# Even mixer of a two-layer backbone: other rates for the work woven into five stages, two modulation pieces one stage later, and the solve's 64-product groups in two rounds

## The chip, the cores and the metric

The kernel runs on one core of one Trainium2 chip. TensorE (PE; its weight loads are PEld), VectorE (DVE), ScalarE (ACT), GpSimd (POOL) and SyncE (SP, which here only issues DMAs) each work through their own instructions in order. The metric is the device time of one execution in microseconds, lower is better. Times are medians of several executions.

## The reference, cut to what matters

The network has two layers. The first is the even layer, with the mixer that the change is in; after each mixer comes a mixture of experts. All numbers are fp32.

```python
mod = silu(c) @ ada_w[i] + ada_b[i]            # 6144 modulation columns for each layer, same for c_ctx
h = rmsnorm(x) * (1 + sc1) + sh1
p = h @ ev_w_in                                # k, v, r, low-rank decay and rate, pool input u
# for each of 8 heads, both directions, context then latent tokens:
S_t = S_{t-1} (diag(w_t) - kk_t^T (a_t kk_t)) + v_t^T k_t ;  y_t = S_t r_t
y = concat([(group_norm(yf + yb) + bonus) * g, pool_mixer(u)]) @ ev_w_out
x = x + g1 * y
```

## The kernel before, in words

The even mixer handles 512 tokens (256 context, 256 latent). The recurrence is computed in 8 chunks of 64 tokens, for two *halves* (4 heads each) and two directions d, so there are four *units* (half, d). For each unit, `ev_prep` makes decays and the products within each chunk, `ev_solve` inverts the triangular 64x64 block of every chunk, and `ev_chain` carries the state through the 8 chunks. Around them are projections of h with `ev_w_in` (`ev_k`, `ev_r`, `ev_v`, `ev_u`), pieces of the modulation (`ev_ada`: one piece is 512 of the columns of `ada_w`, 2 MB in two tiles), transposes (`ev_turn`) and the last steps (`ev_norm`, `ev_bonus`, `ev_pool`, `ev_first`, `ev_last`).

Nothing is scheduled by a compiler: each engine executes in the order in which the Python program issues. Every step is a generator, and a `yield` ends its turn. `weave` (line 109) sets the order. A *round* gives every main generator of a stage one turn, in the order in which they are listed, and then `per` turns, on average, to the *fill*, the generators of the second list, one after the other. When all main generators have ended, what is left of the fill runs alone. `STAGES` (line 356) lists eight stages; each has its main list, its fill, its `per`, and the PSUM banks for the fill and for side products. Two stages never overlap in the program's order.

One turn of `ev_k`, `ev_r`, `ev_v` or `ev_u` is two of eight products of 128x128 by 128x512 (L545). One piece of `ada` (line 261) has three turns with work on TensorE: the first tile (A, L269), the second tile and its copy to SBUF (B, L269, L275), and a small product that turns or picks the result (C, L280 or L289 and L291); what remains of a gate's piece is a DMA by POOL in its next turn. The weight tiles of all fills come in one order (`plan_even` reads the same `STAGES`) through a ring of three slots of 1 MB: when a tile is used up, SP issues the next load.

`ev_solve` goes through 15 rows, two at a time: products with a selection matrix (L802), then per row a multiply and a reduction on VectorE (L808, L809), each row waiting for the one before. Then come four groups of products through `products` (line 821): P1 and P2 with four blocks (64 products, 128 recorded matmuls and 128 weight loads, L825), P3 and P4 with two blocks (64 recorded matmuls). P2 needs a ScalarE copy of P1's result, P3 a VectorE subtraction and transpose of P2's, P4 a copy of P3's. `ev_chain` has three turns for each chunk: *a* (L871, L874, L879 and a ScalarE copy R), *b* (L883, then VU by ScalarE and VectorE, L884 and L885), *c* (L890, L903, then on VectorE the new state ZB, L897, which the next *a* needs at L874). `ev_prep` has 13 turns for each of two quarters: w, a, upto (L690, L697, L703), KB, Kh, RK (VectorE, L720 to L737), an empty one, two transposes (L743), four products (L752, L755).

Of the kernel before, what the change touches and what calls it, by code (L numbers as in the profile page):

```python
# [206 lines left out]
class Kernel:  # L207
# [96 lines left out]
    def mix_in(self, tp, pp, L, x, cols, ahead):  # L304
# [31 lines left out]
        for k in range(8):  # L336
# [11 lines left out]
            if k:  # L348
# [6 lines left out]

    STAGES = (((("kk", 0),), (("k", 0), ("r", 0)), 1.25, "fpPcC", "s"),
              ((("prep", 0, 0),), (("v", 0), ("ada", 1), ("turn", 0), ("ada", 2)), 0.8, "fcC", "s"),
              ((("prep", 0, 1), ("solve", 0, 0), ("bonus", 0)), (("ada", 6),), 1, "fc", "C"),
              ((("chain", 0, 0), ("kk", 1), ("solve", 0, 1)), (("ada", 2), ("k", 1), ("r", 1)), 1, "fp", "P"),
              ((("chain", 0, 1), ("prep", 1, 0)), (("v", 1),), 0.9, "fs", "s"),  # L360
              ((("norm", 0), ("solve", 1, 0), ("prep", 1, 1)), (("ada", 3), ("turn", 1), ("ada", 4)), 1, "fc", "C"),
              ((("solve", 1, 1), ("chain", 1, 0), ("bonus", 1), ("pool",)), (("ada", 1), ("u",), ("ada", 1)), 1, "fp", "P"),
              ((("weights",), ("end",)), (("first",), ("last",)), 0.67, "fpP", "s"))

    def plan_even(self):
# [394 lines left out]
    def ev_solve(self, half, d):  # L760

        nc, c, wp, pp = self.nc, self.c, self.wp, self.pp
        u = self.unit[half, d]
        e, l = (0, 1) if d == 0 else (1, 0)
        G = 16

        KK = u["KK"].rearrange("p (t j) g i -> p t j g i", j=2)
        side = lambda P, a, s: KK[64 * a + P.start:64 * a + P.stop, :, 1 - a, :, s]
        E, Lt = slice(32 * e, 32 * e + 32), slice(32 * l, 32 * l + 32)
        flat = lambda a: a.rearrange("p g i -> p (g i)")  # L770
        both = lambda a, P: a[P].rearrange("p (t g) i -> p t g i", t=4)
        off = lambda P, a: slice(64 * a + P.start, 64 * a + P.stop)
        AT = wp.tile([128, 512], F32, name="AT").rearrange("p (g i) -> p g i", g=G)
        for a in range(2):
            for n, P in enumerate((E, Lt)):
                (nc.scalar.copy if n else nc.vector.tensor_copy)(out=both(AT, off(P, a)), in_=side(P, a, P))
        A32 = wp.tile([128, 512], F32, name="A32").rearrange("p (g i) -> p g i", g=G)
        nc.vector.transpose(flat(A32), flat(AT))
        yield

        nc.scalar.activation(AT[:, :, 16 - 16 * d:32 - 16 * d], AT[:, :, 16 - 16 * d:32 - 16 * d], AF.Copy, scale=c["subcol"][:, d:d + 1])
        nc.gpsimd.memset(AT[:, :, 16 * d:16 * d + 16], 0.0)


        eye = c["eye16"][:, None, :].to_broadcast([128, G, 16])
        A16 = wp.tile([128, G, 16], F32, name="A16")
        nc.vector.scalar_tensor_tensor(A16, A32[:, :, 0:16], c["subcol"][:, 0:1], eye, op0=ALU.mult, op1=ALU.subtract)
        nc.vector.scalar_tensor_tensor(A16, A32[:, :, 16:32], c["subcol"][:, 1:2], A16, op0=ALU.mult, op1=ALU.add)
        X = wp.tile([128, G, 16], F32, name="X")
        nc.scalar.copy(out=X, in_=eye)  # L790
        yield
        yield
        rows = list(range(1, 16) if d == 0 else range(14, -1, -1))
        while rows:
            two, rows = rows[:2], rows[2:]
            ps = pp.tile([128, 2, G, 16], F32, name="s")
            span = lambda i: slice(0, i + 1) if d == 0 else slice(i, 16)
            for j, i in enumerate(two):
                r = span(i)
                for k in range(4):  # L800
                    Q = slice(32 * k, 32 * k + 32)
                    nc.tensor.matmul(ps[Q, j, :, 0:r.stop - r.start], c[f"sel{i}"][Q], A16[Q, :, r], start=j == 0, stop=i == two[-1],  # L802
                                     skip_group_check=True)
            for j, i in enumerate(two):
                r = span(i)
                n = r.stop - r.start
                tmp = wp.tile([128, G, 16], F32, name="tmp")
                nc.vector.tensor_tensor(tmp[:, :, 0:n], ps[:, j, :, 0:n], X[:, :, r], op=ALU.mult)  # L808
                nc.vector.tensor_reduce(X[:, :, i], tmp[:, :, 0:n], axis=AX.X, op=ALU.add)  # L809
                yield  # L810

        TT = wp.tile([128, 512], F32, name="TT").rearrange("p (g i) -> p g i", g=G)
        TN = wp.tile([128, 512], F32, name="TN").rearrange("p (g i) -> p g i", g=G)
        sub = c["sub2"].rearrange("p (s i) -> p s i", s=2)
        nc.scalar.activation(TT[:, :, 16:32], X, AF.Copy, scale=c["subcol"][:, 1:2])
        nc.vector.tensor_tensor(TT[:, :, 0:16], X, sub[:, None, 0, :].to_broadcast([128, G, 16]), op=ALU.mult)
        nc.vector.transpose(flat(TN), flat(TT))
        yield
        yield

        def products(P, L, R, blocks):
            ps = pp.tile([128, G, 32], F32, name="s")
            for g in range(G):
                for lhs, rhs, out in blocks:
                    nc.tensor.matmul(ps[out, g], L(lhs, g), R[rhs, g], start=g == 0, stop=g == G - 1, skip_group_check=True)  # L825
            return ps

        quarters = [(slice(32 * k, 32 * k + 32),) * 3 for k in range(4)]
        ps = products(None, lambda P, g: AT[P, g], TN, quarters)
        M = wp.tile([128, 512], F32, name="A32").rearrange("p (g i) -> p g i", g=G)  # L830
        nc.scalar.copy(out=M, in_=ps)
        yield
        ps = products(None, lambda P, g: M[P, g], TT, quarters)
        nc.vector.tensor_tensor(TT, TT, ps, op=ALU.subtract)
        nc.vector.transpose(flat(TN), flat(TT))
        for a in range(2):
            nc.scalar.copy(out=side(Lt, a, Lt), in_=both(TT, off(Lt, a)))
        yield
        yield

        ee, ll = ([off(P, a) for a in range(2)] for P in (E, Lt))
        ps = products(None, lambda P, g: KK[P, g // 4, 1 - P.start // 64, g % 4, Lt], TN, [(ee[a], ee[a], ll[a]) for a in range(2)])
        M = wp.tile([128, 512], F32, name="A32").rearrange("p (g i) -> p g i", g=G)
        for a in range(2):
            nc.scalar.copy(out=M[ll[a]], in_=ps[ll[a]])
        yield
        ps = products(None, lambda P, g: M[P, g], TT, [(ll[a], ll[a], ee[a]) for a in range(2)])
        for a in range(2):
            nc.scalar.copy(out=side(E, a, E), in_=both(TT, ee[a]))
            nc.vector.tensor_scalar(side(E, a, Lt), both(ps, ee[a]), -1.0, None, op0=ALU.mult)  # L850
        yield
# [1748 lines left out]
```

## Time and profile before

| | us |
|---|---|
| median of the executions shown (1870.68 to 1872.27) | 1871.91 |
| the profiled execution | 1874.16 |
| its span, first to last instruction | 1872.4 |
| of it, the five stages whose rates change (126.2 to 480.6) | 354.4 |

Stages are counted from 1, as they are listed in `STAGES`. In the trace, the third (prep 0,1; solve 0,0) lies at 126.2 to 187.1 us, the fourth (chain 0,0; solve 0,1) at 187.1 to 261.9, the fifth (chain 0,1; prep 1,0) at 261.9 to 325.4, the sixth (norm 0; solve 1,0; prep 1,1) at 325.4 to 400.9, the seventh (solve 1,1; chain 1,0; pool) at 400.9 to 480.6; each begins with the first product of its first main step. The page gives busy shares of every engine in 40 equal slices of the span (46.8 us each) and, below them, the TensorE clock that was granted. A row of the timeline has start, duration, engine, line, operation, tiles, count, and in brackets how long the engine was idle before it and what ended that; "issue" there means that the engine waited for nothing that the profile shows.

### The profile page before, as it was taken

How to read it: one execution, taken by the hardware profiler on the slowest of the kernel's cores; microseconds unless marked ns; L12 is line 12 of the kernel's file. 1: busy time of each engine (PE TensorE's matmuls, PEld its weight loads, DVE VectorE, ACT ScalarE, POOL GpSimd, SP SyncE). 2: the span in 40 equal slices, each digit the busy share in tenths (PEclk: the TensorE clock that was granted, in tenths of full speed). 3: DMA queues.
4: the chain of work that ended last, by engine and by line, in shares of the span. 5: the costliest groups of instructions: out<-in, count | busy, mean ns of one | idle time of the engine just before them, and what ended most of it. 6: DMA issues, size and time to landing. Idle time of an engine off the chain costs nothing. (4 is left out here: it accounts for less than half of the span.)

```text
span 1872.4 us, 31604 instructions
## 1 busy us (share of the span) xinstructions
PE 1637.9 (87%) x12958; PEld 933.3 (50%) x12958; DVE 817.3 (44%) x1622; ACT 447.0 (24%) x945; POOL 139.5 (7%) x170
## 2 busy tenths in 40 slices
PE   5988999989998999999999997999987787776667
PEld 2755556454776444444444433888754333332222
DVE  2564434544358245555555456665562212221113
ACT  3442222421213211111111112544421111111001
POOL 1021000103115000000000003200010000000001
PEclk8998987879898999999999997999988899898888
DMA  9275300652243879999999990622699998999996
GB/s 319 82 239 191 113 24 23 216 172 92 85 146 141 350 283 386 399 385 390 390 401 379 399 386 12 198 68 85 259 369 413 415 415 318 414 414 414 366 400 253
DMA packets 127284, 505.76 MB, mean 270 GB/s; under 512 B 11317, under 2 KB 38945, under 8 KB 85986
## 3 DMA queue, kind: packets, MB, share of 16 engines
q1 hardware_dynamic: 120946, 493.96, 68.1%
q0 software_dynamic: 3488, 8.26, 1.4%
q8 instruction: 143, 2.34, 0.5%
q10 hardware_dynamic: 2640, 0.65, 0.2%
q14 instruction: 67, 0.55, 0.1%
HBM read 501.73 MB, written 1.10 MB: 269 GB/s over the span
## 5 line engine op out<-in xcount | busy, mean ns | idle before, releaser
L1979 PE MATMUL b<-w,ht 128*64 128x512 f32 x512 | 118.8, 604 | 8.6 <-PEq L2197 8.2
L2004 DVE TENSOR_TENSOR tmp<-b,g 128x512 f32<-128x512 f32 x128 | 87.6, 686 | 70.1 <-PE b L2002 69.2
L1958 PE MATMUL b<-w,xh 128*64 128x512 f32 x512 | 116.9, 599 | 0.0
L1958 PE MATMUL b<-w,xg 128*64 128x512 f32 x512 | 116.9, 599 | 0.0
L2287 PE MATMUL b<-w,x 128*32 128x256 f32 x1024 | 77.8, 430 | 31.7 <-DMA w<-moe_w_up 14.9
L2006 DVE TENSOR_TENSOR x<-x,tmp 128x512 f32<-128x512 f32 x124 | 90.1, 726 | 4.3
L2287 PE MATMUL b<-w,xg 128*32 128x256 f32 x1024 | 74.0, 420 | 19.1 <-DMA w<-moe_w_up 14.4
L1987 DVE TENSOR_TENSOR yl<-b,yh 64x512 fp32r<-64x512 f32 x62 | 42.7, 688 | 101.4 <-ACT yh L1986 101.4
L2304 PE MATMUL b<-w,ht 128*32 128x256 f32 x1024 | 71.2, 415 | 16.6 <-ACT ht L2299 12.4
L2292 DVE SCALAR_TENSOR_TENSOR low<-b,gs,low 64x256 f32<-64x256 f32 x32 | 15.7, 490 | 157.6 <-ACT low L2291 157.6
L1979 PEld LDWEIGHTS b<-w,ht 128*64 128x64 f32 x512 | 41.6, 138 | 84.0 <-issue 72.5
L1962 ACT ACTIVATE low<-b 64x512 f32<-64x512 f32 x33 | 19.4, 588 | 253.9 <-PEq L2197 221.0
L2453 DVE COPY y<-b 32x256 f32<-32x256 f32 x62 | 25.9, 418 | 119.6 <-PE b L2304 106.3
L2287 PEld LDWEIGHTS b<-w,x 128*32 128x32 f32 x1024 | 37.1, 122 | 69.5 <-DMA w<-moe_w_up 20.6
L1986 ACT CAST yh<-b 64x512 fp32r<-64x512 f32 x62 | 36.0, 581 | 127.8 <-PE b L1979 104.6
L1963 DVE SCALAR_TENSOR_TENSOR low<-b,gs,low 64x512 f32<-64x512 f32 x32 | 36.1, 1127 | 67.2 <-ACT low L1962 67.2
L1958 PEld LDWEIGHTS b<-w,xh 128*64 128x64 f32 x512 | 33.9, 136 | 62.6 <-issue 62.0
L1958 PEld LDWEIGHTS b<-w,xg 128*64 128x64 f32 x512 | 33.9, 136 | 62.3 <-issue 61.3
L2291 ACT ACTIVATE low<-b 64x256 f32<-64x256 f32 (+1 forms) x36 | 14.4, 399 | 209.9 <-PEq L2501 130.4
L2287 PEld LDWEIGHTS b<-w,xg 128*32 128x32 f32 x1024 | 36.0, 120 | 53.3 <-DMA w<-moe_w_up 19.5
L2002 PE MATMUL b<-yh,oht 128*128 128x512 f32 (+1 forms) x128 | 58.3, 456 | 3.2 <-DVE tmp L2004 3.2
L1374 PE MATMUL b<-w,hH 128*128 128x256 f32 x320 | 59.4, 286 | 0.0
(868 smaller groups left out, 3115.5 us busy)
## 6 DMA issues: line engine op xcount, KB each, us to landing
w<-moe_w_gate SPq DMA_DIRECT2D x128, 1024.0 KB
w<-moe_w_up SPq DMA_DIRECT2D x128, 1024.0 KB
w<-moe_w_down SPq DMA_DIRECT2D x128, 1024.0 KB
w<-ada_w SPq DMA_DIRECT2D x48, 1024.0 KB
w<-od_w_in SPq DMA_DIRECT2D x12, 1024.0 KB
w<-ev_w_in SPq DMA_DIRECT2D x8, 1024.0 KB
w<-ev_w_out SPq DMA_DIRECT2D x5, 1024.0 KB
w<-od_w_out SPq DMA_DIRECT2D x4, 1024.0 KB
```

Of the source, the lines that this page charges most:

```text
L1374: nc.tensor.matmul(ps[:, t], l[:, k, T], r[:, k], start=t == 0 and k == 0 and i == 0, stop=k == 7 and i == 2, skip_group_check=True)
L1958: nc.tensor.matmul(ps[64 * j:64 * j + 64], xe(k), w[j][:, k % 4], start=k == 0, stop=k == 7)
L1963: nc.vector.scalar_tensor_tensor(hs[64:128].rearrange("s k q -> s q k"), ps[64:128].rearrange("s (q k) -> s q k", k=4), gs, sg[64:128].rea ...
L1979: nc.tensor.matmul(ps[64 * j:64 * j + 64], ht[:, k], w[:, k % 2, 512 * j:512 * j + 512], start=k == 0, stop=k == 3)
L1986: nc.scalar.copy(out=yh[:, j], in_=pj)
L1987: nc.vector.tensor_tensor(yl[:, j], pj, yh[:, j].bitcast(F32), op=ALU.subtract)
L2002: nc.tensor.matmul(ps, ohT[0:n, t], y[0:n, j], start=i == 0, stop=i == len(parts) - 1)
L2004: nc.vector.tensor_tensor(tmp, ps, g2[seg[t]][:, 512 * j:512 * j + 512], op=ALU.mult)
L2006: (nc.gpsimd if j in aside else nc.vector).tensor_tensor(xs, xs, tmp, op=ALU.add)
L2287: nc.tensor.matmul(ps[groups[j]], xe(k), w[j // 2][:, k % 4, 256 * (j % 2):256 * (j % 2) + 256], start=k == 0, stop=k == 7, skip_group_che ...
L2304: nc.tensor.matmul(ps[groups[j]], ht[:, k % 2, S * (k // 2):S * (k // 2) + S], w[:, k % 2, 256 * j:256 * j + 256], start=k == 0, stop=k == ...
L2453: (nc.scalar.copy if j % 2 else nc.vector.tensor_copy)(out=out, in_=ps[groups[j]])
```

## The change

Stages three to seven get another `per`, so that their fill lasts for more rounds. Two pieces of `ada` (layer 1, pieces 1 and 2: column pieces that no DMA writes out, first read in the odd mixer) go from the head of the fourth stage's fill to the end of the fifth's; the weight stream's order follows. And `products` becomes a generator: with more than two blocks it yields once halfway, so P1 and P2 take two rounds each; P3 and P4 stay as they are. No arithmetic and no transfer is added or removed.

```diff
-              ((("prep", 0, 1), ("solve", 0, 0), ("bonus", 0)), (("ada", 6),), 1, "fc", "C"),
-              ((("chain", 0, 0), ("kk", 1), ("solve", 0, 1)), (("ada", 2), ("k", 1), ("r", 1)), 1, "fp", "P"),
-              ((("chain", 0, 1), ("prep", 1, 0)), (("v", 1),), 0.9, "fs", "s"),
-              ((("norm", 0), ("solve", 1, 0), ("prep", 1, 1)), (("ada", 3), ("turn", 1), ("ada", 4)), 1, "fc", "C"),
-              ((("solve", 1, 1), ("chain", 1, 0), ("bonus", 1), ("pool",)), (("ada", 1), ("u",), ("ada", 1)), 1, "fp", "P"),
+              ((("prep", 0, 1), ("solve", 0, 0), ("bonus", 0)), (("ada", 6),), 0.65, "fc", "C"),
+              ((("chain", 0, 0), ("kk", 1), ("solve", 0, 1)), (("k", 1), ("r", 1)), 0.6, "fp", "P"),
+              ((("chain", 0, 1), ("prep", 1, 0)), (("v", 1), ("ada", 2)), 0.5, "fs", "s"),
+              ((("norm", 0), ("solve", 1, 0), ("prep", 1, 1)), (("ada", 3), ("turn", 1), ("ada", 4)), 0.82, "fc", "C"),
+              ((("solve", 1, 1), ("chain", 1, 0), ("bonus", 1), ("pool",)), (("ada", 1), ("u",), ("ada", 1)), 0.8, "fp", "P"),
...
             for g in range(G):
+                if g == G // 2 and len(blocks) > 2:
+                    yield
                 for lhs, rhs, out in blocks:
...
-        ps = products(None, lambda P, g: AT[P, g], TN, quarters)
+        ps = yield from products(None, lambda P, g: AT[P, g], TN, quarters)
...
-        ps = products(None, lambda P, g: M[P, g], TT, quarters)
+        ps = yield from products(None, lambda P, g: M[P, g], TT, quarters)
```

The two-block calls get the same `yield from`. Counted from the yields of the generators, with the round of the last fill turn:

| stage | rounds before | fill turns, last in round | rounds after | fill turns, last in round |
|---|---|---|---|---|
| third | 27 | 18, in 18 | 28 | 18, in 28 |
| fourth | 26 | 22, in 22 | 28 | 16, in 27 |
| fifth | 27 | 8, in 9 | 27 | 14, in 26, one behind the main steps |
| sixth | 27 | 23, in 23 | 28 | 23, in 27, one behind the main steps |
| seventh | 26 | 22, in 22 | 29 | 22, in 28 |

## Rows read from the trace of the kernel before

**Rows 1.** The page's 40 slices: TensorE's busy tenths, then its granted clock.
```profile
PE   5988999989998999999999997999987787776667
...
PEclk8998987879898999999999997999988899898888
```

**Rows 2.** Busy time of each engine in the five stages (first line names the columns).
```profile
core 0: us, PE busy (x) PEld busy (x) DVE busy (x) ACT busy (x) POOL busy (x), PEclk, DMA share, GB/s
126.20:187.10 60.90, 50.59 (x808) 30.60 (x808) 35.23 (x74) 19.59 (x37) 9.51 (x17) 0.87 0.65 221
187.10:261.90 74.80, 70.96 (x962) 39.37 (x961) 33.78 (x87) 17.47 (x38) 0.36 (x2) 0.93 0.27 86
261.90:325.40 63.50, 60.41 (x447) 40.63 (x445) 26.21 (x57) 16.73 (x35) 2.35 (x5) 0.80 0.06 18
325.40:400.90 75.50, 66.30 (x887) 38.60 (x886) 38.04 (x80) 27.29 (x48) 6.94 (x13) 0.79 0.58 196
400.90:480.60 79.70, 74.37 (x957) 39.27 (x956) 35.63 (x86) 19.57 (x43) 21.27 (x35) 0.91 0.41 132
```

**Rows 3.** The same view of the six stretches with the clock at half.
```profile
165.00:171.80 6.80, 4.07 (x97) 2.60 (x101) 5.07 (x11) 1.09 (x2) 0.00 (x0) 0.50 0.38 144
178.60:192.30 13.70, 13.70 (x185) 9.34 (x186) 7.03 (x14) 5.02 (x11) 0.36 (x2) 0.50 0.12 28
257.10:270.80 13.70, 12.39 (x146) 7.69 (x141) 2.10 (x4) 5.48 (x9) 0.00 (x0) 0.50 0.06 24
308.30:339.10 30.80, 29.94 (x145) 19.56 (x146) 11.88 (x25) 8.64 (x19) 1.21 (x3) 0.50 0.19 62
383.40:403.90 20.50, 19.13 (x305) 13.96 (x305) 7.60 (x14) 6.74 (x13) 0.67 (x2) 0.50 0.25 82
468.80:485.80 17.00, 15.78 (x217) 11.30 (x212) 3.79 (x8) 7.12 (x14) 4.46 (x7) 0.50 0.51 153
```

**Rows 4.** TensorE's waits, 126.2 to 480.6: total us, times, longest.
```profile
PE s L825 <- issue: 8.5, 3, 4.2
...
PE C L920 <- DVE sq L916: 4.3, 2, 3.7
...
PE p L752 <- issue: 1.6, 1, 1.6
```

**Rows 5.** Timeline of TensorE: P2 in the sixth, seventh and fourth stage.
```profile
384.77 1.49 PE L825 MATMUL s<-TT,A 32*32 32x32 f32 x93 [4.23 <-issue]
...
468.11 0.50 PE L825 MATMUL s<-TT,A 32*32 32x32 f32 x35 [3.24 <-issue]
...
250.17 1.29 PE L825 MATMUL s<-TT,A 32*32 32x32 f32 x128
```

**Rows 6.** DMA queues inside the stall, 380.6 to 384.7: packets, MB, share.
```profile
q1 hardware_dynamic: 651, 1.28, 93.5%
q8 instruction: 1, 0.02, 1.7%
```

**Rows 7.** The same between P1 and P2 of the fourth stage, 246.9 to 250.2.
```profile
q8 instruction: 1, 0.02, 2.3%
```

**Rows 8.** Timeline of TensorE: two hand-overs of the chain, fifth stage without fill.
```profile
305.96 0.65 PE L890 MATMUL C<-VU,tok 128*64 128x64 f32 x6 [1.09 <-ACT VU L884]
...
308.53 0.70 PE L874 MATMUL c<-ZB,RK 128*64 128x128 f32 x4 [1.18 <-DVE ZB L897]
```

**Rows 9.** Timeline of TensorE: second row pair of the solve, third and sixth stage.
```profile
136.41 0.45 PE L802 MATMUL s<-A,const_sel 32*32 32x64 f32 x16 [1.29 <-DVE tmp L808]
...
344.07 0.46 PE L802 MATMUL s<-A,const_sel 32*32 32x64 f32 x16 [1.69 <-DVE tmp L808]
```

**Rows 10.** Timeline of TensorE: one fill turn of a projection, one of `ada`.
```profile
206.42 1.98 PE L545 MATMUL f<-x,w 128*128 128x512 f32 x4
...
129.30 1.06 PE L269 MATMUL f<-w,sT 128*32 128x512 f32 x8
```

More of the change, by code (lines that the diff above doesn't have):

```diff
@@ L841, in ev_solve @@
         ee, ll = ([off(P, a) for a in range(2)] for P in (E, Lt))
-        ps = products(None, lambda P, g: KK[P, g // 4, 1 - P.start // 64, g % 4, Lt], TN, [(ee[a], ee[a], ll[a]) for a in range(2)])
+        ps = yield from products(None, lambda P, g: KK[P, g // 4, 1 - P.start // 64, g % 4, Lt], TN, [(ee[a], ee[a], ll[a]) for a in range(2)])
         M = wp.tile([128, 512], F32, name="A32").rearrange("p (g i) -> p g i", g=G)
@@ L846, in ev_solve @@
         yield
-        ps = products(None, lambda P, g: M[P, g], TT, [(ll[a], ll[a], ee[a]) for a in range(2)])
+        ps = yield from products(None, lambda P, g: M[P, g], TT, [(ll[a], ll[a], ee[a]) for a in range(2)])
         for a in range(2):
```

## Prediction

> **What bounds the kernel now.** I began with the 40 slices [rows 1]. Slices three to eleven hold the stages that change. TensorE is busy 8 to 9 tenths there, so at first sight it is full; but the clock line below it dips to 7 and 8, so part of "busy" is the same work at half speed. Next I cut the span at the stage borders [rows 2]. In 354.4 us TensorE is busy 322.6 and idle 31.8; no other engine passes six tenths of a stage (VectorE in the third: 35.2 of 60.9), and the DMA share is 0.65 at most. So TensorE's order bounds all five stages, in two ways: gaps, and the clock. For the clock I took the six stretches at 0.50 [rows 3]: TensorE is busy 95.0 us in them, of which 5.2 lie after 480.6. At full speed the 89.8 us inside would be some 45. The same work without gap and at full clock would take 322.6 - 44.9 = 277.7 us: the five stages lose 76.7 us, 31.8 to gaps and 44.9 to the clock. This is what the change can draw on. What follows (last mixer stage, experts, odd layer) depends on the end of the seventh stage, so a gain here should reach the end one to one.
>
> Then the causes. Each drop of the clock follows gaps that lie close together, at places where the fill has run out or the solve's products run: 3.7 us before L920 ahead of 165.0 [rows 4]; an "issue" wait of 1.6 us at L752, and shortly before it one of 1.0 at L825 (8.5 less the two of [rows 5]), ahead of 178.6 [rows 4]; two gaps of 1.09 and 1.18 us around 305 to 308.5 ahead of 308.3, in rounds with no fill [rows 8]; 4.23 and 3.24 us inside P2 ahead of 383.4 and 468.8 [rows 5]. Single gaps of 1.29 and 1.69 us [rows 9] were followed by no drop.
>
> **Part 1, the instruction stalls.** "Issue" waits at L825 and L752 are 8.5 + 1.6 = 10.1 us [rows 4]. In the one of 4.23 us, the instruction queue moved a single packet of 0.02 MB while the weight queue held 93.5% of the DMA engines [rows 6]; in the fourth stage the same packet went out between P1 and P2 with nothing else in flight, and P2 ran through in 1.29 us [rows 5, 7]. I read this as TensorE running out of instructions: P1 and P2 are 256 instructions each in 1.3 us, and the next block comes late behind weight loads. Halving P1 and P2 puts a round between groups of 128, some 2.3 us (60.9 us over 27 rounds in the third stage). That slows the demand to about half, but a block that takes 4 us or more to come is not covered wholly. I take 5 us of the 10.1 as gained; bounds 0 and 9.
>
> The Trainium skill, in "Runtime: NRT & Kernel Launch", section "Instruction fetch mechanics", says that instructions are fetched ahead in blocks of 16 KB and that this stays hidden, since dispatch is slower than the fetch. The trace of before does not agree: the wait of 4.23 us holds just such a packet [rows 5, 6]. By the page, nothing of this part is gained; that is the third rival.
>
> **Part 2, gaps in rounds that now get fill.** Fourth stage, rounds 23 to 26: its whole idle time, 74.8 - 71.0 = 3.8 us [rows 2], lies almost all there. Afterwards fill turns of 1.98 us [rows 10] stand in rounds 24, 26 and 27 and cover the copies between P2, P3 and P4: I leave 0.5. Fifth stage, rounds 10 to 27: idle 63.5 - 60.4 = 3.1 us [rows 2]; half the rounds get a turn: 1.5 left. Seventh: of its 5.3 us [rows 2], 3.2 are part 1, some 1.2 are P4 and the chain after round 22: 0.5 left. Sum: 5 us gained; bounds 2 and 6. The 3.7 us before L920 stay: there VectorE works without a break on prep's KB and Kh and the solve's last rows, and the round behind Kh has no fill either way.
>
> **Part 3, gaps in rounds that lose their fill.** The fill that is spread is taken from the rounds that had one each. Cover goes where nothing else stands behind a hand-over of the chain: after *b* (wait for VU, 1.09) or *c* (wait for ZB, 1.18) [rows 8]. Counting rounds, those are in the fourth stage 5, 15 and 20 in full, 3, 8 and 23 in part (some 4.7 us), in the fifth 5 (17 is in part 2), in the seventh 11: 7 us. After *a*, L879 covers the copy. In the third and sixth stage the second row pair waits for VectorE [rows 9]; VectorE's work there is unchanged, so taking one turn of 1.06 us [rows 10] away adds at most that, and where TensorE got there earlier for having less to do, less. I take 1 us for both. Sum: 8 us lost; bounds 3 and 14. The two `ada` pieces only change stage: the same TensorE work, no POOL DMA, no early reader, and in the fifth stage, whose DMA share is 0.06 [rows 2], room for their four loads. The weight loads on SP keep their order of use; those for the mixer's last stage queue behind tiles that are used later than before, but several rounds still lie between. I cost this at 0; without that cover it would be one 1 MB load, under 5 us at the 221 GB/s of the third stage [rows 2], which the range has room for. The turns left behind the main steps (fifth and sixth stage) are TensorE work at its usual price.
>
> **Part 4, the clock.** Half of the busy time in [rows 3] is lost: 2.0, 6.9, 6.2, 15.0, 9.6 and 7.9, sum 47.5 us (2.6 after 480.6). No row says which drops go, so this is bounded by counting drops. The shortest full ones lasted 13.7 us and cost up to 6.9 [rows 3]. Those at 257.1 and 308.3 follow tails without fill and should go, and the second, 30.8 us long and begun in rounds of short products alone, should at least be shorter, with turns of `ada` among them. Those at 383.4 and 468.8 go if part 1's stalls become short. The one at 165.0 stays. New ones may come where prep's VectorE work and a thinned fill meet: rounds 5 to 7 of the third, 5 to 8 of the sixth stage. I take four drops of 6.9 afterwards, the one at 165.0 among them: 27.4 in place of 47.5, so 20 us gained; bounds 0 (seven drops) and 34 (two).
>
> **Sum.** -5 - 5 + 8 - 20 = -22 us. Against the profiled execution (span 1872.4, its own time 1874.16, so 1.8 outside the span): 1852. The median of the runs shown is 2.25 below that time: 1850. With the favourable ends but few new gaps (-5, -6, +5, -34): -40, 1832.
>
> **Rivals.** First, slower: *the clock falls at every prep.* Mechanism: in rounds KB and Kh of `ev_prep`, VectorE has some 3 us and more of work for a solve or chain that TensorE waits for; until now each round had a fill turn in front of that wait. With two turns in three rounds (one in two in the fifth stage) the gaps [rows 8, 9] double up and each pair ends in a drop. For it: [rows 8], where two gaps close together did this. Against it: 1.69 alone did not [rows 9]. Price: eight drops (two each in third, fifth and sixth stage, the two P2) x 6.9 = 55 in place of 47.5, new gaps 14, gained 5 + 4: +12, about 1884. It decides from the point where more than six or seven drops remain.
>
> Second, no change: *the idle time only moves.* Gaps return one for one (part 3 at 14, parts 1 and 2 at 10), and the drops move with them, saving less than one: 1872, give or take 3.
>
> Third, *the split does nothing*: the waits come from something else, or the blocks still come too late. Then the 10.1 us stay, and so do the drops at 383.4 and 468.8. I had counted 5 us and, of those two drops, about 9: -22 + 14 = -8, 1864. For it: the weight queue fills the DMA engines for the whole stall [rows 6], and a split does not change what it loads. Against it: the quiet fourth stage, where the packet came in time [rows 5, 7]. The page of the Trainium skill named in part 1 would lead here too: fetch that is always hidden leaves the split nothing to hide.
>
> That the change doesn't do what it says is excluded by the round counts: the fill ends in the last rounds of each stage.
>
> **Chances.** Forecast case (1832 to 1862) 0.61; slower 0.17; no change 0.10; the split does nothing 0.12. A measurement of this kernel can tell about 0.2%, 4 us, from no change. Faster: 0.61 + 0.12 = 0.73; same 0.10; slower 0.17. For the range, I leave out the best end of the forecast case (0.07, below 1830) and most of the slower case (0.13, above 1874): 1830 to 1874.
>
> **What would show it.** Part 1: "issue" waits at L825 under 6 us in sum, and none above 3. Part 2: no gap over 0.7 us behind P2 in the fourth stage. Part 3: new gaps of about 1.1 us at L890 and L874 in rounds 5, 15 and 20 of the fourth stage. Part 4: half-clock time from 126 us to the end of the seventh stage of 50 to 60 us in place of 97; 257.1 and 308.3 without a counterpart. The prediction is wrong if half-clock time stays above 80 us, if VectorE's share rises above two thirds in the third or sixth stage with TensorE waiting for it, or if the experts start earlier by the gain and the end does not move.

## The result, and the profile after

| | us |
|---|---|
| before, median of 4 executions | 1871.30 |
| the changed kernel, median of 4 (1884.83 to 1889.46) | 1887.32 |
| ratio | 1.0093 [1.0068, 1.0117] |
| its profiled execution, and its span | 1884.83, 1883.0 |
| measured again beside 35 executions of before, 12 executions | 1880.27, ratio 1.0066 [1.0039, 1.0093] |

The kernel became slower by 0.7 to 0.9%, 12 to 17 us by the ratios, where 22 us of gain had been forecast. The forecast of 1850 and its range are both missed. A few executions of the experiments ran in a much slower state (two of one kernel, and one of the last, its profiled one) and are left out of every figure.

Lines from 821 on stand two lower in the code (L825 is now L827, L920 L922, L2311 L2313). First the busy time of each engine in the five stages, in the same columns as [rows 2]:

```profile
core 0: us, PE busy (x) PEld busy (x) DVE busy (x) ACT busy (x) POOL busy (x), PEclk, DMA share, GB/s
129.00:199.40 70.40, 56.55 (x808) 32.00 (x808) 36.14 (x78) 19.80 (x37) 10.42 (x17) 0.80 0.55 181
199.40:271.20 71.80, 67.37 (x904) 37.89 (x904) 31.71 (x81) 15.85 (x35) 0.35 (x2) 0.91 0.08 26
271.20:341.00 69.80, 62.41 (x502) 39.04 (x501) 27.79 (x61) 18.30 (x39) 2.35 (x5) 0.90 0.23 76
341.00:408.40 67.40, 58.97 (x887) 33.07 (x887) 38.98 (x83) 27.26 (x49) 6.37 (x12) 0.90 0.66 221
408.40:484.60 76.20, 71.72 (x950) 36.54 (x950) 32.77 (x81) 17.24 (x39) 17.53 (x29) 0.96 0.35 118
```

The third stage, with the same 808 matmuls, takes 70.4 us in place of 60.9; the sixth is 8 us shorter; the fifth holds the moved `ada` pieces (502 matmuls, 455 before). Here the borders are the first products of the main steps; by that rule the fifth stage before begins at 261.3 us and the eighth at 479.4, where [rows 2] have 261.9 and 480.6. Over all five, 355.6 us, TensorE is busy 317.0 us and idle 38.6; before, with the same borders, it is 353.2, 321.9 and 31.3. So some clock was gained, but idle time grew.

The half-clock stretches, to be held against [rows 3]:

```profile
140.90:144.30 3.40, 3.40 (x10) 0.70 (x10) 2.68 (x7) 0.00 (x0) 0.00 (x0) 0.50 0.00 0
168.20:175.10 6.90, 5.67 (x74) 2.18 (x77) 3.53 (x7) 0.64 (x2) 1.15 (x2) 0.51 0.27 73
181.90:205.80 23.90, 21.20 (x284) 13.68 (x271) 8.01 (x17) 7.04 (x14) 1.48 (x4) 0.50 0.29 93
236.50:243.30 6.80, 6.56 (x43) 3.55 (x44) 4.25 (x9) 2.48 (x4) 0.00 (x0) 0.50 0.26 99
...
sum 75.30, PE 69.95 PEld 35.05 DVE 27.68 ACT 17.31 POOL 3.78; mean PE 7.77 PEld 3.89 DVE 3.08 ACT 1.92 POOL 0.42
```

There are nine, 75.3 us in sum (97 within the five stages before). In this profile the long ones at 308 and 383 have gone, and the one at the end of the third stage has grown from 13.7 to 23.9 us.

Second, a place that the prediction did not look at: the last 35 us, far behind the change. TensorE's timeline of after, then of before:

```profile
1842.02 3.49 PE L1818 MATMUL b<-xh,const_ident 128*128 128x512 f32 x6
1851.02 0.66 PE L2313 MATMUL b<-const_ident,oh 128*128 128x128 f32 x2 [5.51 <-PEq L2503]
1852.14 0.47 PE L2300 MATMUL b<-const_ident,low 64*128 64x64 f32 x2 [0.46 <-ACT oht L2314]
1852.97 3.64 PE L2306 MATMUL b<-w,ht 128*32 128x256 f32 x32 [0.35 <-ACT ht L2301]
```

```profile
1842.48 0.41 PE L2311 MATMUL b<-const_ident,oh 128*128 128x128 f32 x2 [0.30 <-PEq L2501]
1843.41 0.30 PE L2298 MATMUL b<-const_ident,low 64*128 64x64 f32 x2 [0.52 <-ACT oht L2312]
1844.07 1.93 PE L2304 MATMUL b<-w,ht 128*32 128x256 f32 x32 [0.36 <-ACT ht L2299]
```

L2503 is the conditional around a skipped expert; "PEq" is TensorE's sequencer. The branch takes 5.51 us in place of 0.30, and the 32 matmuls behind it run at half clock (3.64 us in place of 1.93). From that product to the end of the span it takes 32.0 us (29.9 before). So 5.2 + 2.1 = 7.3 us are lost here, though nothing was changed here. Inside the gap the DMA queues moved this:

```profile
q1 hardware_dynamic: 381, 2.22, 98.4%
q8 instruction: 1, 0.02, 1.2%
```

It is the picture of [rows 6]: one instruction packet behind a full weight queue.

### The profile page after: what moved, and what is told of

Read it like the earlier page. It is cut to its first block, busy times and chain, and to the rows that moved or that the text cites. A ratio compares the mean times of both kernels' runs of the same rounds, so it can differ in the third digit from the quotient of the medians.

```text
span 1883.0 us, 31599 instructions
## 1 busy us (share of the span) xinstructions
PE 1641.9 (87%) x12958; PEld 926.2 (49%) x12958; DVE 816.2 (43%) x1622; ACT 447.1 (24%) x945; POOL 140.8 (7%) x170
## 5 line engine op out<-in xcount | busy, mean ns | idle before, releaser
L2289 PE MATMUL b<-w,xg 128*32 128x256 f32 x1024 | 75.6, 431 | 16.5 <-DMA w<-moe_w_up 13.7
L2306 PE MATMUL b<-w,ht 128*32 128x256 f32 x1024 | 75.6, 443 | 13.3 <-ACT ht L2301 12.5
```

What stands on the lines that cost most here:

```text
L2289: nc.tensor.matmul(ps[groups[j]], xe(k), w[j // 2][:, k % 4, 256 * (j % 2):256 * (j % 2) + 256], start=k == 0, stop=k == 7, skip_group_che ...
L2306: nc.tensor.matmul(ps[groups[j]], ht[:, k % 2, S * (k // 2):S * (k // 2) + S], w[:, k % 2, 256 * j:256 * j + 256], start=k == 0, stop=k == ...
```

## The experiments

Theory: the loss has two places, the branch in the tail (where the instructions lie in their blocks) and the third stage (fill taken from where it was free). Rivals: the tail waits for data; the drops of the clock merely move between stages; the split itself costs. Each kernel ran beside 31 to 35 executions of the kernel before on its own chip. Drains stand in for missing instructions: the change makes TensorE's program five instructions shorter (26,415 instructions of TensorE are recorded before, weight loads included, and 26,410 after), and they are put behind the even mixer.

| kernel | executions | median us | ratio to before |
|---|---|---|---|
| changed, five drains | 12 | 1877.57 | 1.0045 [1.0026, 1.0065] |
| before, 251 drains | 10 | 1879.30 | 1.0051 [1.0027, 1.0074] |
| split alone | 12 | 1872.11 | 1.0018 [0.9996, 1.0040] |
| all rates, no split | 12 | 1877.64 | 1.0043 [1.0023, 1.0063] |
| rates 4 to 7, no split | 12 | 1871.69 | 1.0024 [1.0001, 1.0047] |
| the same again | 10 | 1875.12 | 1.0058 [1.0031, 1.0085] |
| rates 4 to 7 and split (third put back) | 12 | 1863.44 | 0.9972 [0.9950, 0.9994] |
| changed, third at 0.8 | 12 | 1867.20 | 0.9997 [0.9974, 1.0020] |
| changed, third early | 12 | 1863.53 | 0.9973 [0.9951, 0.9995] |
| third at 0.65 alone | 11 | 1876.16 | 1.0046 [1.0020, 1.0072] |
| third at 0.65 and split | 9 | 1881.56 | 1.0070 [1.0045, 1.0096] |
| rates 6 and 7 and split | 12 | 1865.76 | 0.9987 [0.9966, 1.0007] |
| third put back, fourth 0.7 | 12 | 1863.63 | 0.9970 [0.9948, 0.9992] |
| the same, sixth and seventh 0.9 | 12 | 1863.15 | 0.9969 [0.9950, 0.9988] |
| third early, fourth 0.7, sixth 0.9 | 12 | 1860.78 | 0.9966 [0.9945, 0.9987] |

Executions of one kernel differ by 10 to 25 us here, so verdicts rest on ratios and on lengths seen in many profiles, never on the end time of one profile.

### The tail: numbers of instructions

```diff
 x = K.even(xp, seg)
 consts = ctx.enter_context(tc.tile_pool(name="consts2", bufs=1))
+for _ in range(5):
+    tc.nc.tensor.drain()
```

> The changed kernel, with five extra one-instruction drains of TensorE between the even mixer and the first experts, so that every later TensorE instruction has the same number in the program as in the kernel before. Theory 'layout': the 5.51 us gap of TensorE behind a skipped expert in the last 30 us is an instruction block that is not yet there at a branch target, and comes only from the shift by five instructions. Then the gap falls to under 1 us (before: 0.30), the half clock after it goes, and the time falls from 1887 by about 7, to 1880 (profiled against profiled: 1885 to 1878); the even mixer stays as it is. Rival 'weights': the gap has to do with data that arrive late, and comes back whatever the numbering: 1887, gap 4 to 6 us.

Measured: 1.0045, and TensorE's timeline at that place:

```profile
1853.46 0.41 PE L2313 MATMUL b<-const_ident,oh 128*128 128x128 f32 x2 [0.30 <-PEq L2503]
1854.39 0.30 PE L2300 MATMUL b<-const_ident,low 64*128 64x64 f32 x2 [0.52 <-ACT oht L2314]
1855.05 1.93 PE L2306 MATMUL b<-w,ht 128*32 128x256 f32 x32 [0.35 <-ACT ht L2301]
```

Five instructions that compute nothing remove the gap and the half clock behind it. The theory holds; "weights" falls.

The opposite, in the kernel before, at the start of the program:

```diff
+for _ in range(251):
+    tc.nc.tensor.drain()
 dp = ctx.enter_context(tc.tile_pool(name="mod", bufs=1, space=bass.MemoryType.DRAM))
```

> The kernel before with 251 one-instruction drains of TensorE at its very start, where TensorE waits until 8.96 us for its first data: every later TensorE instruction is then numbered, within blocks of 256, as behind the even mixer of the changed kernel (251 = 256 - 5). Theory 'layout': the gap behind the skipped expert (0.30 us before, 5.51 after) becomes 4 to 6 us with half clock behind it, and the time rises by about 7, plus what the drains delay the first product: 1868 to about 1876. Rival 'the even mixer's change brings the gap about': the gap stays at 0.30 us and the time at 1868 to 1870.

Measured: 1.0051, and

```profile
1838.75 0.66 PE L2311 MATMUL b<-const_ident,oh 128*128 128x128 f32 x2 [5.54 <-PEq L2501]
```

The gap appears in a kernel whose mixer was not touched. So it belongs to the position of the branch in the instruction stream: 5 fewer and 251 more do the same, as blocks of 256 instructions (or of a divisor of it) would make them. Other shifts were not tried. In all 14 profiles in which TensorE has as many recorded instructions as before, the branch takes 0.30 us. From the end of the seventh stage to the end of the span it takes 1398.4 to 1399.3 us in the three profiles with the gap and 1384.2 to 1393.0 in the others, so the loss is not given back at another branch. Such waits are no oddity of this place, though: the kernel before, too, waits 5.5 us for TensorE's sequencer at one product (L2287, 122 us before its end), and each of the 17 profiles has 7 to 12 such waits of over 1 us behind the mixer. The Trainium skill, "Runtime: NRT & Kernel Launch", section "Instruction fetch mechanics", says that a taken branch to a target outside the fetched window has to wait for a DMA fetch; the traces agree (the gap of 5.51 us holds an instruction packet, the one of 0.30 us before holds none, both beside a full weight queue), and put the price at 5.2 us here.

> The changed kernel itself, beside the same runs of the kernel before as the other three, since the difference to its copy with five drains (ratio 1.0045) is so far taken across chips. Theory 'the shifted instruction numbers cost the difference': ratio 1.008 to 1.010, gap behind the skipped expert 5 to 6 us, against 0.30 in the other three. Rival 'the first comparison overstated it': ratio 1.004 to 1.006 in spite of the gap.

The changed kernel unaltered. Measured: 1.0066, between the two theories; the gap is there (5.67 us). The interval reaches from 1.0039 to 1.0093, so by medians alone the shift costs 0.2 to 0.5%; the 7.3 us of the trace are 0.4%.

### The third stage

```diff
-(("bonus", 0)), (("ada", 6),), 0.65, "fc", "C"),
+(("bonus", 0)), (("ada", 6),), 1, "fc", "C"),
```

> The changed kernel with the third stage's rate put back to 1 (as before), the other four stages as changed; one drain keeps the instruction numbers behind the even mixer as before. Theory 'VectorE-bound rounds need their fill early': the third stage goes from 70.4 us back to about 61, its waits of 2.65 us behind the row pair and of 4.11 us at the end shrink to at most 1.5 and 3.7, and with the gap of the last 30 us gone too, the time is 1887 - 7 - 9 = 1871, a little below the kernel before if its first start is equal. Rival 'the drops only move': the third stage gains 9 and the fourth loses most of it: 1876 to 1880.

Measured: 0.9972, 5 us below the kernel before; the stage takes 59.5 us. Against the changed kernel with drains (1.0045) that is 0.73%, 13.6 us, for one number. To see why, cut the stage at its second product of `sq` (L920, L922; `sq` is made in round 18, behind Kh, and used in round 20). Before, then after:

```profile
126.20:167.70 41.50, 33.93 (x382) 16.81 (x382) 27.52 (x63) 14.22 (x28) 9.51 (x17) 0.97 0.94 323
167.70:187.10 19.40, 16.66 (x426) 13.79 (x426) 7.72 (x13) 5.37 (x9) 0.00 (x0) 0.68 0.01 3
```

```profile
129.00:169.40 40.40, 30.04 (x326) 15.12 (x326) 27.36 (x62) 12.98 (x25) 9.01 (x15) 0.94 0.67 225
169.40:199.40 30.00, 26.51 (x482) 16.87 (x482) 8.78 (x17) 6.81 (x12) 1.41 (x3) 0.61 0.39 120
```

Up to that product TensorE has 56 matmuls less to do (326 in place of 382; six fill turns: four of eight matmuls at 1.06 us [rows 10] and two short ones, some 6 us), yet gets there only 1.1 us sooner. The second part gets those 56 matmuls and is 10.6 us longer, at clock 0.61. TensorE's timeline names what held the first part:

```profile
139.30 0.45 PE L802 MATMUL s<-A,const_sel 32*32 32x64 f32 x16 [2.65 <-DVE tmp L808]
...
169.43 2.08 PE L922 MATMUL C<-sq,const_heads 128*128 128x512 f32 x2 [4.11 <-DVE sq L918]
```

The second row pair starts 10.28 us after the stage's first product (139.30 - 129.02); before, it was 136.41 - 126.17 = 10.24 [rows 9]. In 16 of the 17 profiles read it is 10.24 to 10.29 (10.56 at rate 0.8), however much fill stands ahead of it. VectorE, with ScalarE, sets that time: in after it stands still twice on the way, both times for ScalarE,

```profile
130.84 0.43 DVE L694 TENSOR_SCALAR lw<-lw 128x512 f32<-128x512 f32 x1 [1.00 <-ACT lw L693]
...
136.68 0.69 DVE L725 TENSOR_TENSOR KB<-th,kT 128x512 f32<-128x512 f32 x1 [1.07 <-ACT th L724]
```

and the wait of TensorE grew from 1.29 to 2.65. So the fill of the first 18 rounds had been nearly free, and a turn that is moved behind them has to be paid for. By the clock of the trace, the 10.6 us of the second part are 5.7 us of moved work at full clock, 4.1 us lost to the clock (20.8 us of TensorE's busy time there are at half clock, 12.6 before) and 0.8 us of idle time.

```diff
-(("bonus", 0)), (("ada", 6),), 1, "fc", "C"),
+(("bonus", 0)), (("ada", 6),), 0.65, "fc", "C"),
```

(In the kernel before; the second of the two also has the split.)

> The kernel before with the third stage's rate at 0.65 alone (no split, nothing else changed; four drains keep the later numbers). Theory 'the third stage costs by itself': it is 8 to 11 us longer (61.0 before), and the time 1.004 to 1.007 of before. Rival 'without the split it costs little': 1.000 to 1.003, the stage at 65 us or less, or given back in the fourth.

> The kernel before with the third stage's rate at 0.65 and the split, all other rates as before; four drains. Theory 'the effects add': split alone 1.0018, third stage 0.7% on top: 1.006 to 1.010. Rival 'with its fill spread over the halves the third stage is no loss': 1.000 to 1.003.

Measured: 1.0046 and 1.0070; the stage takes 71.4 and 72.6 us. Without the split, the first:

```profile
127.10:167.30 40.20, 29.83 (x326) 15.12 (x326) 27.39 (x62) 12.98 (x25) 9.04 (x15) 0.94 0.65 227
167.30:198.50 31.20, 27.04 (x482) 17.30 (x482) 8.77 (x16) 6.81 (x12) 1.41 (x3) 0.61 0.36 116
```

The same split into 40 and 31 us: the third stage costs by itself, and both theories that said so hold. Over the six profiles with 0.65 the stage takes 66.6 to 72.8 us (mean 70.7), over nine with 1 it takes 59.3 to 62.9 (mean 60.2).

```diff
-(("bonus", 0)), (("ada", 6),), 0.65, "fc", "C"),
+(("bonus", 0)), (("ada", 6),), 0.8, "fc", "C"),
```

> The changed kernel with the third stage's rate at 0.8 in place of 0.65 (1 before): its 18 fill turns end in round 23, not 28 or 18; two drains keep the later numbers. Theory 'thinned fill in front of VectorE's row pairs costs by degrees': the third stage takes about 65 us (61 at 1, 67 to 73 at 0.65) and the time lies midway, 1867 to 1873. Rival 'any thinning brings the clock down early in the stage': as at 0.65, 1875 to 1879. Rival 'only the last rounds matter': as at 1, 1861 to 1865.

Measured: 0.9997 and 64.6 us: by degrees.

```diff
+    n = 0
     while main:
         main = [g for g in main if next(g, end) is not end]
-        due += per
+        n += 1
+        due += per if per != 0.65 else 1 if n <= 6 else 0.56
```

> The changed kernel, with the third stage's fill one turn a round for the first six rounds, as before, and then thin (0.56 a round) to the last round 28; seven drains keep the later numbers. Theory 'the third stage loses at its first row pairs, where VectorE is late': the early waits (2.65, 1.15, 0.71 and 0.63 us, the drop at 137 to 144 us) shrink to those of before (1.29 and 0.55), the stage takes 61 to 63 us, and the time is near that of the third stage put back, 1862 to 1866. Rival 'it loses in its last rounds, where the clock stays down for 14 to 27 us': the early waits shrink but the stage still takes 65 us and more: 1870 to 1875.

Measured: 0.9973, with 62.5 us, cut at the same product:

```profile
130.00:170.90 40.90, 33.07 (x334) 15.90 (x334) 27.47 (x62) 13.07 (x25) 8.41 (x15) 0.85 0.69 231
170.90:192.50 21.60, 18.70 (x474) 13.22 (x474) 8.67 (x17) 6.72 (x12) 1.12 (x2) 0.82 0.58 185
```

The total came out as forecast, but not by the way that was named: the first part is as long as ever, the wait at the second row pair only went to 1.90, and only eight matmuls more were done by then. What is shorter is the second part, 21.6 us at clock 0.82: the last drop began at 188.9 us, 18.0 us behind the `sq` product (12.5 in after). One profile stands behind this; why the drop came later is open. It also bounds what the moved work explains: five of the six turns still lie behind the `sq` product here, and over twelve executions nothing is lost (0.9973, beside 0.9972 with the stage put back). So moving the turns is not enough for the loss; the time at half clock behind them belongs to it, and what sets that is not shown.

### Split and rates

```diff
-                if g == G // 2 and len(blocks) > 2:
-                    yield
```

(Taken out for "no split"; for "split alone" kept, with the rates of before.)

> The kernel before with the split of the 64-product groups alone; all rates and the two ada pieces as before. Its TensorE program is as long as that of the kernel before, so the last 30 us should show no new gap under any theory. Theory 'instruction supply': the issue waits inside P1 and P2 (8.5 us at this line before) fall under 2, the drops of the clock behind them (at 383 and 468 us) go, and the time falls by 8 to 14, to about 1860. Rival 'gaps only': the waits go, but the clock falls anyway a little later because the rounds around it are thin: 1865 to 1869. Rival 'no effect': the waits stay at 8 us and the time at 1871.

> The kernel before with the new rates and the moved ada pieces alone, without the split; seven one-instruction drains of TensorE behind the even mixer keep the later instruction numbers as before. Theory 'the rates cost, the split pays': the third stage grows by 8 to 10 us as in the changed kernel, the issue waits inside P1 and P2 come back in two or three places (6 to 10 us), and the time is above the kernel before by 5 to 12: 1877 to 1883. Rival 'the rates are worth something, the third stage alone is an accident': within 3 us of before, 1868 to 1874.

Measured: 1.0018 and 1.0043 (third stage 72.8 us). For the split alone 'no effect' holds; for the rates alone the waits, the stage and the time came as the theory said, but not that the split pays: with it the ratio is 1.0045 (changed, five drains). TensorE's "issue" waits at the products, 126 to 480 us, for the split alone, the rates alone, and both (the third put back); 8.5 in [rows 4], 1.4 in after:

```profile
PE s L827 <- issue: 7.9, 6, 3.0
```

```profile
PE s L825 <- issue: 7.8, 4, 3.0
```

```profile
PE s L827 <- issue: 1.7, 2, 1.1
```

Neither half of the change does anything to their sum; together they remove six of eight microseconds. The timeline of P2 in the seventh stage, first with the split alone, then with both:

```profile
464.86 0.72 PE L827 MATMUL s<-TT,A 32*32 32x32 f32 x61
468.38 0.31 PE L827 MATMUL s<-TT,A 32*32 32x32 f32 x3 [2.80 <-issue]
```

```profile
443.33 0.75 PE L827 MATMUL s<-TT,A 32*32 32x32 f32 x64
444.01 0.45 PE L885 MATMUL c<-R,AB 64*64 64x64 f32 x8
444.39 1.13 PE L1014 MATMUL P<-th,y 128*128 128x512 f32 x2
445.35 1.88 PE L545 MATMUL p<-x,w 128*128 128x512 f32 x4
447.16 0.75 PE L827 MATMUL s<-TT,A 32*32 32x32 f32 x64
```

With the old rates the fill has run out when P2 comes, so a yield puts few and short products between the halves. With the new ones, four wide products of 1.88 us stand there. That few instructions that take long give the next block its time fits this, but is not shown by it, because the new rates also move the weight loads away from here. The same stretch with the split alone, with both, and with the new rates but P2 undivided (the kernel that comes next; the last two columns are the DMA share and GB/s):

```profile
464.80:468.70 3.90, 1.10 (x72) 0.88 (x68) 0.87 (x2) 0.27 (x1) 3.11 (x5) 0.88 1.02 398
```

```profile
443.30:447.90 4.60, 4.60 (x145) 2.71 (x145) 0.29 (x1) 0.96 (x2) 1.10 (x2) 1.00 0.11 26
```

```profile
463.60:466.90 3.30, 1.52 (x131) 1.38 (x132) 2.00 (x5) 0.00 (x0) 0.14 (x3) 1.00 0.03 5
466.64 0.25 PE L825 MATMUL s<-TT,A 32*32 32x32 f32 x3 [1.76 <-issue]
```

So with a quiet queue alone the wait shrinks (3.24 us in [rows 5]) but stays; with the split and the wide products as well it goes. No run has the split and the wide products beside a full queue in this stage. In the sixth stage the split alone has turns of `ada` (L269, 1.06 us) between the halves of P1 and behind them too, and waits 1.11 and 2.96 us all the same.

That these are waits for instructions is shown better than the prediction had it. From 126 to 500 us, the 17 profiles have 52 "issue" waits of TensorE of over 0.5 us, and every one ends 1.2 to 1.55 us after a packet of the instruction queue q8 has ended. A full weight queue is not needed: in the kernel before, this is all that the DMA queues moved from 170 to 178 us, where TensorE waits 0.99 us at L825 and 1.63 at L752:

```profile
q8 instruction: 2, 0.03, 1.8%
```

The next two, one kernel twice, are "all rates, no split" with the third stage's rate at 1.

> The kernel before with the new rates of stages four to seven and the moved ada pieces; the third stage's rate and the undivided groups of 64 products as before; three drains keep the later numbers. It is the kernel with the third stage put back (1863 beside 1868 of before) without the split. Theory 'split and rates need each other': issue waits inside P1 and P2 return (6 to 8 us from 126 to 500 us, against 1.7 with both) and with them drops, so 1869 to 1873. Rival 'the split is worth nothing': the waits return, but time stays with the rates, 1861 to 1866.

> The new rates of stages four to seven without the split and with the third stage as before, a second time (first: 1.0024). Theory 'the rates of four to seven pay only with the split': again 1.001 to 1.004, beside 0.9972 with the split. Rival 'the first value was a high draw': 0.997 to 0.999.

Measured: 1.0024 and 1.0058, beside 0.9972 with the split; issue waits 5.1 and 6.4 us. With the third stage at 1 the theory "need each other" holds: with the rates of four to seven the split is worth some 0.5 to 0.9%, without them nothing. The same cannot be said with the third stage at 0.65 (1.0043 without, 1.0045 with the split); that these do not add up is left open. Nor is the whole gain a matter of instructions: the seventh stage takes 80.3 us without the split and 75.6 with it (means of the table below), and of these 4.7 us some 2.6 are another wait, for VectorE's `th` in the pool. Without the split, then with it:

```profile
PE P L1012 <- DVE th L1007: 4.2, 1, 4.2
```

```profile
PE P L1014 <- DVE th L1009: 1.5, 1, 1.5
```

### Where the new rates pay

The split, and of the rates only these (in the kernel before):

```diff
-(("ada", 3), ("turn", 1), ("ada", 4)), 1, "fc", "C"),
+(("ada", 3), ("turn", 1), ("ada", 4)), 0.82, "fc", "C"),
...
-(("ada", 1), ("u",), ("ada", 1)), 1, "fp", "P"),
+(("ada", 1), ("u",), ("ada", 1)), 0.8, "fp", "P"),
```

> The kernel before with the split and the new rates of the sixth and seventh stage alone; third, fourth and fifth stage as before, the ada pieces unmoved. Theory 'sixth and seventh hold the gain' (profiled lengths 75.5 and 78.6 us before, 63.8 and 74.2 with the third stage put back): 1862 to 1866, as with the third put back. Rival 'the fourth and fifth stage hold it, through their half-clock time (35.9 us before, 13.4 with the third put back)': 1868 to 1872, as with the split alone.

Measured: 0.9987, between the theories (0.9972 and 1.0018), not told apart by the medians. Lengths of stages over all profiles tell more (first product to first product, in the timelines; the number of profiles behind the comma):

| stage | old rate | new rate, no split | new rate, split |
|---|---|---|---|
| fourth and fifth | 138.0, 6 | 139.7, 3 | 138.9, 6 |
| sixth | 70.2, 5 | 72.1, 3 | 68.5, 8 |
| seventh | 79.9, 5 | 80.3, 3 | 75.6, 8 |

The seventh, through the split, holds most of the gain: 4.3 us. Its eight lengths with both (74.2 to 76.7 us) lie below all eight without (78.6 to 81.0). Fourth and fifth give nothing, and the sixth's lengths spread too widely (63.8 to 75.5 us) for its 1.7 us to be told from nothing.

```diff
-(("k", 1), ("r", 1)), 0.6, "fp", "P"),
+(("k", 1), ("r", 1)), 0.7, "fp", "P"),
```

> The kernel with the third stage put back (split, new rates of four to seven, third at 1; 1863 beside 1868 of before), and the fourth stage's rate at 0.7 in place of 0.6: its 16 fill turns end in round 23, not 27; one drain keeps the later numbers. Theory 'fill into the last round makes the next stage wait': the 2.06 us of TensorE at the fifth stage's first projection (for VectorE's rT, made from the last fill turn) goes to under 0.5, the fourth's hand-over gaps of 1.13 and 1.96 us go or halve, idle time of the fourth and fifth stage falls from 11.4 to about 8, and the time by about 3: 1860. Rival 'the last rounds need the fill more': new gaps of 1 us and more in rounds 24 to 28 of the fourth stage eat this: 1863 to 1867.

Measured: 0.9970; the same as without that edit. The wait named in the theory, and what came in its place (with the third put back, then with 0.7 as well):

```profile
258.61 1.13 PE L690 MATMUL p<-wup,wdT 65*128 65x128 f32 x8 [2.06 <-DVE rT L583]
```

```profile
255.41 1.92 PE L827 MATMUL s<-TN,AB 32*32 32x32 f32 x64 [2.71 <-DVE TN L837]
258.63 1.92 PE L827 MATMUL s<-TT,A 32*32 32x32 f32 x64 [1.31 <-ACT A L847]
```

The rival holds: a wait of 2.06 at the border against 2.71 + 1.31 at P3 and P4 without fill.

On top of that, and then the combination (the third stage's early fill, fourth at 0.7, sixth at 0.9, seventh at 0.8):

```diff
-(("ada", 3), ("turn", 1), ("ada", 4)), 0.82, "fc", "C"),
+(("ada", 3), ("turn", 1), ("ada", 4)), 0.9, "fc", "C"),
...
-(("ada", 1), ("u",), ("ada", 1)), 0.8, "fp", "P"),
+(("ada", 1), ("u",), ("ada", 1)), 0.9, "fp", "P"),
```

> As the one with the fourth stage at 0.7, and the sixth and seventh stage at 0.9 (0.82 and 0.8 in the change, 1 before): their fill ends two and three rounds sooner; two drains. Theory 'each stage needs some rounds between its last fill and the next stage': the waits of 0.76 and 0.41 us at the border of the sixth and seventh stage and of 1.53 and 1.71 us at the end of the seventh go, 3 to 4 us more: 1857. Rival 'clock': the clock's drops at the solves' products return and the time is 1862 to 1868.

> The changed kernel with the third stage's fill one a round for six rounds and thin after that, the fourth stage's rate 0.7 and the sixth's 0.9; seven drains. Each of these alone gave 0.997 of before. Theory 'they add': 0.993 to 0.996, 1856 to 1861. Rival 'each only takes what the others take too, since the clock's drops move between the stages': 0.996 to 0.998, 1862 to 1865.

Measured: 0.9969 and 0.9966. Of the first, the rival 'clock' came out: the wait of 1.53 us for `th` is gone, but one of 1.21 us ("issue", L827) has come, TensorE spends 12.6 us of the seventh stage at half clock (6.8 with the fourth at 0.7 alone), and the time is no better. The rival of the last one holds: single gains of 0.3% do not add up (the sixth at 0.9 had been run only together with the seventh). It is the fastest kernel found, some 6 us below the kernel before and 19 below the changed one by the ratios, but not to be told from the simplest repair (third stage back at 1, one drain).

## Why the prediction was wrong

The account, in means over profiles: third stage +10.5, fourth and fifth +0.9 (138.9 less 138.0), sixth -1.7, seventh -4.3, tail +7.3, sum +12.7 us. Measured: 12.3 (1.0066) and 17.4 (1.0093) of 1869 to 1871. Only the third stage, the seventh and the tail stand clear of the spread between profiles.

- **What bounds the kernel.** The step that failed first. From [rows 2] I concluded that TensorE's order bounds all five stages, since no other engine passes six tenths. In the third stage VectorE's 35.2 us are not spread evenly: 27.5 of them lie in the first 41.5 us, in a chain of short steps that TensorE waits for. The waits in [rows 4] and [rows 9] had it (L802 and L920, both behind VectorE); I read them as single gaps. One of them I also put in the wrong order: the 3.7 us before L920 run from 164.0 to 167.7, so the drop at 165.0 begins inside that gap and not behind it, and so does the one at 383.4 inside the wait of 4.23.
- **Part 3.** Its term for the third and sixth stage together, 1 us, was "at most one turn of 1.06 us". The third alone cost 10.5. I priced the waits that grow (1.29 to 2.65, 3.71 to 4.11; all gaps of its first part together, 7.6 to 10.4) and not the work that lost its free place and was done later: 5.7 us at full clock in the second part, and 4.1 more lost to the clock there. The new gaps of the fourth stage came, but two in place of three: 1.13 us at L892 and 1.96 at L876.
- **Part 1.** The direction was right, and the size too small: the issue waits at L825 and L752 fell from 10.1 us to 1.2 to 2.3 in three profiles of the new mixer (waits of over 0.5 us), against 5 forecast. The reason was half of it. That TensorE runs out of instructions is borne out, but the block does not come late only behind weight loads (1.0 and 1.6 of the 10.1 us had a quiet queue), and a round between the halves is not enough: what stands in it, and the quieter queue, count as well. "The split does nothing", the third rival, is refuted with the new rates and true without them.
- **Part 2.** No gap above 0.7 us stands behind P2 in the fourth stage, as forecast, but a wait of 2.06 us at the next stage's first projection took its place.
- **Part 4.** I forecast 20 us less loss to the clock, and half-clock time of 50 to 60 us. This largest term of the sum failed: it took the drops of one profile for fixed places. Within the five stages, the time at half clock is 75, 73 and 91 us in three profiles of the new mixer, and 96 and 74 in two of the old one (the second with 251 drains), so no gain is shown. TensorE's idle time there, forecast to fall by 2 us (-5 - 5 + 8), rose by 6: 37.3 to 38.6 us, against 31.3 and 32.4. Over twelve executions the mean granted clock is 0.925 with the change (five drains) and 0.925 before. With the third put back it is 0.934, with 31 us at half clock in its one profile.
- **The first rival** came near in time (1884) and sign. Its place was only partly right: VectorE-bound rounds with thinned fill, yes, but in the third stage alone and by moved work; fifth and sixth showed no such loss. That its price came near is luck: it was made of 55 us lost to the clock, and the profile of after has some 35 (half of the 69.95 us that TensorE is busy at half clock).
- **The tail** was in no case. I had taken the layers behind the mixer as following one to one. Behind the mixer 1398 to 1399 us follow in place of 1384 to 1393, since five instructions less put one branch in another place.

## What to carry to other kernels

Before fill is spread out, cut the stage at its waits and ask for each part which engine sets its length; fill in rounds that another engine bounds was nearly free here, and spreading it out made it cost. Look for an instruction packet shortly before the end of an "issue" wait: a group of many tiny products can run out of instructions beside idle DMA queues, and a break in it did nothing by itself. Take no place of a clock drop from a single profile. After any edit ahead of run-time branches, compare the waits at those branches as well: a few instructions that do nothing can be worth more than the edit.

## What was not expected of the hardware

- Five instructions more or less, far ahead, decide whether one branch takes 0.30 or 5.51 us (5.54 and 5.67 in two other kernels).
- 251 drains of TensorE at its start put its first product off from 8.96 to 18.91 us and still cost nothing further on: the waits for the first weights (5.04 us before the second product of the kernel before) take it up, and the third stage starts at 126.1 us with them and at 126.2 without.
- All 52 "issue" waits of over 0.5 us in the 17 profiles end 1.2 to 1.55 us after an instruction packet, 17 of them with the DMA engines idle (share 0.00; the longest of these took 1.76 us).
- Executions of one and the same kernel range over 17 us (1861.28 to 1878.71 for before, 35 executions), and mean clock and time go together within a kernel (correlation -0.47 to -0.85 in each of the 16 sets of executions of the other kernels; for before -0.57 to -0.66 in three sets and 0.0 in a fourth): with drops that start or not, one profile says little about a stage's length.
